# The opening of a hybrid decoder block laid in another order: where the first loads, transposes and small tables stand

## The chip, the cores and the metric

One core of a Trainium2 chip runs the whole kernel. The metric is the device time of one execution in microseconds (us). Three runs of the kernel before took 2296.9, 2298.59 and 2299.16 us; the median is 2298.59. A core has five engines that run their own instruction streams in the order laid down at build time: TensorE (PE; its weight loads are shown apart as PEld), VectorE (DVE), ScalarE (ACT), GpSimd (POOL) and SyncE (SP, which here only asks for transfers). Transfers (DMA) are asked for by SyncE or GpSimd and run beside the engines.

## The reference

One decoder layer over x of 512 tokens by 2048 channels, all float32. Cut to what matters here:

```python
mod = silu(c) @ w_ada + b_ada                # 2048 -> 6 x 2048, one row
shift1, scale1, gate1, shift2, scale2, gate2 = split(mod, 6)
h = rms_norm(x, norm1_w) * (1 + scale1) + shift1
proj = h @ w_in                              # 2048 -> 7168 columns
aq, ak, av, gq, gf, gi, gg = split(proj)     # seven blocks of 1024
attn = dilated_attention(rope(rms(aq)), rope(rms(ak)), av)   # 8 heads
ho = hgrn2(gq, gf, gi, lb)                   # 8 heads, lb from softmax(hg_lb_logits)
x = x + gate1 * (concat(norm(attn), gated(ho)) @ w_out)
x = x + gate2 * (relu(h2 @ w_ff1)**2 @ w_ff2)                # h2: x normalised and modulated again
```

Before any product with `w_in`, x must be normalised by the root mean square of each token, turned so that channels lie on the 128 partitions, and scaled by `norm1_w * (1 + scale1)`. `scale1` itself is a product of a vector with 16 MB of `w_ada`.

## The kernel before

**Precision and products.** Each float32 operand of a large product is split into a rounded part `hi` and a rest `lo`; a product is three matmuls (hi·hi, lo·hi, hi·lo). Weights are split on the fly: ScalarE casts `whi` (L39), VectorE subtracts `wlo` (L40). The input chunk k (128 channels of 512 tokens) is split into `hhi[k]`, `hlo[k]`.

**Opening.** `crow` takes c, norm1_w and b_ada; TensorE turns it (L82), and ScalarE and VectorE make `sc` = silu(c) (L88, L89). Rows of other small vectors go by GpSimd's queue into the tile `rows` (L94 to L97), which shares its place with `crow`; between its clearing (L92) and those requests GpSimd's stream holds the clearing of a part of `wcol` (L107), a tile that a transfer has filled before.

**Modulation rows.** `gemv` (L116) forms one block of `mod`: it asks for pieces of `w_ada` of 256 KB (SyncE, L123) and VectorE multiplies and adds them with `sc` as per-partition scalars into two accumulators (L127, L129). `to_cols` then sums over partitions by TensorE transposes (L149) and ScalarE copies that accumulate (L152); VectorE adds the bias (L167) and forms `norm1_w * (1 + scale1)` (L169) in `g1c`. scale1 has eight blocks of 256 columns, each serving two chunks k; shift1 has four blocks of 512.

**x.** Sixteen pieces of x (`xs[ti][q]`, L255) are asked for behind the eight pieces of scale block 0. Squares are summed on ScalarE, two of sixteen on VectorE (L261, L264); `rx`, the reciprocal root, is a power on GpSimd (L212). All of x is scaled by `rx` (L277 ScalarE, two pieces; L279 VectorE, fourteen) and turned by 64 transposes (L283) into `xnT[0..15]` (L285), all written ahead of the first product.

**First two groups.** `first_groups` (L288) multiplies pairs of chunks with 512 columns of `gf` and 256 of `gq`, 16 chunks by 18 matmuls; before each pair, `scale_block` (L303) runs a block of scale1 and `scaled` (L332) makes `hhi`, `hlo` of the pair. The first products are unshifted: what shift1 adds is made apart by `shift_through` (L744), a `gemv` of `w_in` with shift1. During the second group `shift_block` steps through the blocks of shift1 and then `shifted` (L339) adds it to the chunks. From project(5120) on (L833) TensorE's order is the written one; all else is ordered at build time by a planner that takes instructions as they become ready by its own timeline, earlier written ones first. `issue_after(ins)` lays the instructions of a block behind `ins` on that engine's stream. A pool with n buffers makes a load wait until one is free.

**Small tables.** Behind the last `g1c` step stand `posf`, the transposes of `rows` (L768, L769), the softmax for `lb` (one exp), and sine and cosine for the rotation (L766 to L818), then eight products on GpSimd (`rot_w`, L822). ScalarE loads a function table ahead of the exp and of the sine.

Of the kernel before, what the change touches and what calls it, by code (L numbers as in the profile page):

```python
# [15 lines left out]
P = 128  # L16
# [28 lines left out]
def hybrid_block(ctx, tc, x, c, positions, norm1_w, w_ada, b_ada, w_in, q_norm_w, k_norm_w,  # L45
# [29 lines left out]
    pool.memset(mhalf, -0.5)  # L75
# [10 lines left out]
    dve.tensor_copy(bcol, ps_c[:, 2 * NK:P])  # L86
    sc = const.tile([P, NK], F32, name="sc")
# [28 lines left out]
    def gemv(view, vec, col0, n=512, early=False):  # L116
# [3 lines left out]
        for k0 in range(0, NK, nk):  # L120
            raw = spare.pop(0) if early and spare else slot("araw") if early else gv.tile([P, 512], F32, name="araw", bufs=4)
            raw = raw.rearrange("p (k n) -> p k n", n=n)
            nc.sync.dma_start(raw, view[:, k0:k0 + nk, col0:col0 + n])  # L123
            for k in range(k0, k0 + nk):
                acc = accs[k % 2]
                if k < 2:
                    dve.tensor_scalar(acc, raw[:, k - k0], vec[:, k:k + 1], None, op0=ALU.mult)  # L127
                else:
                    dve.scalar_tensor_tensor(acc, raw[:, k - k0], vec[:, k:k + 1], acc, op0=ALU.mult, op1=ALU.add)  # L129
# [8 lines left out]
    def to_cols(accs, dst):  # L138

        nb = accs[0].shape[1] // P  # L140
        parts = 1 if nb == 4 else 2
        if parts == 1:
            dve.tensor_tensor(accs[0], accs[0], accs[1], op=ALU.add)
        yield
        pc = bank("pc")
        for j in range(nb):
            for u in range(parts):
                c = (j * parts + u) * P
                pe.transpose(pc[:, c:c + P], accs[u][:, j * P:(j + 1) * P], ident)  # L149
        for j in range(nb):  # L150
            c = pc[:, j * parts * P:(j + 1) * parts * P]
            act.activation(c, c, AF.Copy, accum_out=dst[:, j:j + 1])  # L152
# [7 lines left out]
    def mod_cols(kind, b, dst, nw, n=512, early=False):  # L160

        for _ in gemv(ada_v, sc, kind * D + b * n, n, early):
            yield
        nb = n // P
# [3 lines left out]
        if nw is not None:  # L168
            mod_cols.last = dve.scalar_tensor_tensor(d, d, 1.0, nw[:, b * nb:(b + 1) * nb], op0=ALU.add, op1=ALU.mult)  # L169
# [16 lines left out]
    def load_w(view, k0, c0, n=512, eng=None, ahead=True, raws=None):  # L186
        with tc.high_priority() if ahead else ExitStack():
            raw = wr.tile([P, 2, n], F32, name="wraw", tag="raw", bufs=4)
            nc.sync.dma_start(raw, view[:, k0:k0 + 2, c0:c0 + n])
# [20 lines left out]
    def rstd_of(dst, ss, n, inv_n):  # L210
        dve.tensor_scalar(dst, ss, inv_n, EPS, op0=ALU.mult, op1=ALU.add)
        pool.tensor_tensor(dst, dst, mhalf[:, 0:n], op=ALU.pow)  # L212
# [34 lines left out]
    first_scale = mod_cols(1, 0, g1c, n1c, 256, True)  # L247
    for _ in range(8):
# [7 lines left out]
    for q in range(4):  # L256
        for ti in range(NT):
            jk = work("jk")
            with tc.issue_after(sc_ready.ins), tc.issue_after(sig_ready.ins):
                if q == 3 and ti % 2:  # L260
                    dve.tensor_tensor_reduce(jk, xs[ti][q], xs[ti][q], op0=ALU.mult, op1=ALU.add, scale=1.0, scalar=0.0,  # L261
                                             accum_out=ssx[:, ti, q:q + 1])
                else:
                    act.activation(jk, xs[ti][q], AF.Square, accum_out=ssx[:, ti, q:q + 1])  # L264
    dve.tensor_reduce(rx, ssx, axis=AX.X, op=ALU.add)
    rstd_of(rx, rx, NT, 1.0 / D)
    run_all(first_scale)
    second_scale = mod_cols(1, 1, g1c, n1c, 256, True)
# [4 lines left out]
    xnT = []  # L273
    for q in range(4):
        for ti in range(NT):
            if q == 0 and ti % 2 == 0:
                act.activation(xs[ti][q], xs[ti][q], AF.Copy, scale=rx[:, ti:ti + 1])  # L277
            else:
                dve.tensor_scalar(xs[ti][q], xs[ti][q], rx[:, ti:ti + 1], None, op0=ALU.mult)  # L279
        for j in range(4):  # L280
            pt = bank("ptx")
            for ti in range(NT):
                pe.transpose(pt[:, ti * P:(ti + 1) * P], xs[ti][q][:, j * P:(j + 1) * P], ident)  # L283
            t = slot("xnT")
            act.copy(t, pt)  # L285
            xnT.append(t)

    def first_groups(c_f, c_q, before, after):  # L288
# [1131 lines left out]
```

## Time and profile before

The span is the time from the first to the last instruction of one profiled execution; the execution's own time is a little longer.

| what | value |
|---|---|
| median of three runs | 2298.59 us |
| profiled execution, its own time | 2297.95 us |
| its span | 2296.2 us |
| TensorE busy | 2224.9 us (97%) |
| VectorE busy | 1809.9 us (79%) |
| ScalarE busy | 1098.2 us (48%) |
| GpSimd busy | 447.3 us (19%) |
| DMA moved | 598.31 MB, mean 261 GB/s |
| share of the ending chain | PE 60%, DVE 17%, DMA 14%, issue 6% |

A row of the timeline gives start, duration, engine, line, operation, tile written and tiles read, count, and in brackets the idle time ahead of it with what ended it. A group's row gives busy time and the mean of one in ns, then idle time ahead. Busy time of TensorE is that of overlapping matmuls, so one matmul's duration is longer than the distance between two starts.

### The profile page before, as it was taken

The page shows a single profiled execution, that of the slowest core. Times are in us where ns is not written, and L with a number is a line of the kernel's source. Part 1 is how long each engine was busy: PE and PEld are TensorE (multiplying, and loading weights), DVE is VectorE, ACT ScalarE, POOL GpSimd, SP SyncE. Part 2 cuts the span into 40 slices and gives each one's busy share as a digit, 9 for nine tenths or more (in the row PEclk, how much of TensorE's full clock was granted, in tenths as well). Part 3 has the DMA queues.
Part 4 walks back from the last instruction along what each step waited for, and adds up shares of the span by engine and source line. Part 5 has one row for each costly group of instructions (what it writes and reads, how often), then busy time and mean ns, then how long its engine had stood idle before and what let it go on. Part 6 is the DMA issues. An engine that isn't in the chain of part 4 may idle for free.

```text
span 2296.2 us, 33105 instructions
## 1 busy us (share of the span) xinstructions
PE 2224.9 (97%) x11769; PEld 1824.4 (79%) x11769; DVE 1809.9 (79%) x2765; ACT 1098.2 (48%) x1950; POOL 447.3 (19%) x664
## 2 busy tenths in 40 slices
PE   4899999999999999999999999999999999999999
PEld 3787877888778888778887888888888888888887
DVE  6999777677876565668648988988897679967878
ACT  5555434433344454447544556555564333343332
POOL 1000022000230000002232323323332222222221
PEclk9999999999999999999999999999999999999999
DMA  9798455556545256746969799889889987998784
GB/s 327 254 335 315 124 177 156 177 160 207 187 151 184 68 173 225 247 152 217 367 231 383 251 344 347 298 306 386 298 328 390 339 293 260 385 344 291 278 301 164
DMA packets 262582, 598.31 MB, mean 261 GB/s; under 512 B 23220, under 2 KB 43968, under 8 KB 262416
## 3 DMA queue, kind: packets, MB, share of 16 engines
q1 hardware_dynamic: 186800, 332.54, 43.1%
q0 software_dynamic: 70720, 254.21, 30.0%
q10 hardware_dynamic: 4896, 9.44, 1.2%
q8 instruction: 93, 1.52, 0.3%
q14 instruction: 73, 0.60, 0.1%
HBM read 518.49 MB, written 77.61 MB: 260 GB/s over the span
## 4 chain that ended last, share of the span: by engine, by line
PE 60%; DVE 17%; DMA 14%; issue 6%; ACT 2%; POOL 1%; SPq 0%; DVEq 0%; ACTq 0%; POOLq 0%
PE f L1177 9%; PE f L1178 9%; PE f L1176 9%; DMA araw<-in_w_ada_dram 6%; PE prj L198 5%; PE prj L199 5%; PE prj L200 5%; DVE vlo L1161 3%; DVE acc L129 3%; DVE raw L1144 2%; PE f L208 2%; PE f L206 2%; PE f L207 2%; DMA Fl<-f_lod 2%; DVE wlo L40 2%
## 5 line engine op out<-in xcount | busy, mean ns | idle before, releaser
L1160 ACT CAST vhi<-raw 128x1024 fp32r<-128x1024 f32 x392 | 413.4, 1055 | 534.5 <-PE f L1178 416.3
L1161 DVE TENSOR_TENSOR vlo<-raw,vhi 128x1024 fp32r<-128x1024 f32 x392 | 475.5, 1219 | 153.5 <-ACT vhi L1160 152.7
L1177 PE MATMUL f<-vlo,Fh 128*128 128x512 f32 x1376 | 537.1, 390 | 3.9 <-DVE vlo L1161 3.8
L1178 PE MATMUL f<-vhi,Fl 128*128 128x512 f32 x1376 | 535.8, 389 | 0.8 <-DMA Fl<-f_lod 0.8
L1176 PE MATMUL f<-vhi,Fh 128*128 128x512 f32 x1376 | 536.1, 390 | 0.0
L39 ACT CAST whi<-wraw 128x512 fp32r<-128x512 f32 (+1 forms) x368 | 219.8, 601 | 453.2 <-PE prj L200 313.3
L198 PE MATMUL prj<-whi,hi 128*128 128x512 f32 x896 | 364.9, 407 | 1.3 <-ACT gg L701 1.3
L200 PE MATMUL prj<-whi,lo 128*128 128x512 f32 x896 | 351.4, 392 | 0.0
L199 PE MATMUL prj<-wlo,hi 128*128 128x512 f32 x896 | 351.0, 392 | 0.0
L40 DVE TENSOR_TENSOR wlo<-wraw,whi 128x512 fp32r<-128x512 f32 (+1 forms) x368 | 243.2, 665 | 120.9 <-ACT whi L39 118.3
L129 DVE SCALAR_TENSOR_TENSOR acc<-araw,sc,acc 128x512 f32<-128x512 f32 (+1 forms) x392 | 252.7, 672 | 100.5 <-DMA araw<-in_w_ada_dram 99.2
L1177 PEld LDWEIGHTS f<-vlo,Fh 128*128 128x128 f32 x1376 | 258.3, 188 | 63.3 <-DVE vlo L1161 10.0
L1178 PEld LDWEIGHTS f<-vhi,Fl 128*128 128x128 f32 x1376 | 258.3, 188 | 54.8 <-DMA Fl<-f_lod 1.6
L1176 PEld LDWEIGHTS f<-vhi,Fh 128*128 128x128 f32 x1376 | 258.3, 188 | 53.5
L1144 DVE TENSOR_TENSOR raw<-raw,raw 128x1024 f32<-128x1024 f32 x224 | 267.7, 1216 | 4.1 <-DMA raw<-in_w_ff_dram 3.9
L198 PEld LDWEIGHTS prj<-whi,hi 128*128 128x128 f32 x896 | 169.3, 189 | 36.5 <-ACT gg L701 1.6
L200 PEld LDWEIGHTS prj<-whi,lo 128*128 128x128 f32 x896 | 168.9, 188 | 36.7
L199 PEld LDWEIGHTS prj<-wlo,hi 128*128 128x128 f32 x896 | 169.5, 189 | 33.0 <-DVE wlo L40 1.0
L1122 POOL DMA_DIRECT2D Fh<-f_hid x112 | 79.0, 705 | 425.9 <-PE f L1178 410.8
L208 PE MATMUL f<-hi,wlo 128*128 128x512 f32 x256 | 99.8, 390 | 1.3 <-DVE wlo L40 1.3
L206 PE MATMUL f<-hi,whi 128*128 128x512 f32 x256 | 100.2, 391 | 0.0
L207 PE MATMUL f<-lo,whi 128*128 128x512 f32 x256 | 99.6, 389 | 0.0
(311 smaller groups left out, 2917.0 us busy)
## 6 DMA issues: line engine op xcount, KB each, us to landing
raw<-in_w_ff_dram SPq DMA_DIRECT2D x224, 512.0 KB, 9.7
araw<-in_w_ada_dram SPq DMA_DIRECT2D x384, 256.0 KB, 4.3
Fh<-f_hid POOLq DMA_DIRECT2D x112, 512.0 KB, 6.5
Fl<-f_lod POOLq DMA_DIRECT2D x112, 512.0 KB, 7.7
wraw<-in_w_in_dram SPq DMA_DIRECT2D x104, 512.0 KB, 4.1
Fh<-h_hid POOLq DMA_DIRECT2D x60, 512.0 KB, 6.6
Fl<-h_lod POOLq DMA_DIRECT2D x60, 512.0 KB, 7.5
f_hid<-part POOLq DMA_DIRECT2D x48, 512.0 KB, 7.9
```

Source lines behind the costliest of these rows:

```text
L39: nc.scalar.copy(hi, src)
L40: (eng or nc.vector).tensor_tensor(lo, src, hi.bitcast(F32), op=ALU.subtract)
L129: dve.scalar_tensor_tensor(acc, raw[:, k - k0], vec[:, k:k + 1], acc, op0=ALU.mult, op1=ALU.add)
L198: pe.matmul(banks[ti], lhsT=hi[:, ts], rhs=whi, start=first, stop=False)
L199: pe.matmul(banks[ti], lhsT=hi[:, ts], rhs=wlo, start=False, stop=False)
L200: pe.matmul(banks[ti], lhsT=lo[:, ts], rhs=whi, start=False, stop=last)
L1144: dve.tensor_tensor(dst, a, b, op=ALU.subtract)
L1160: act.copy(hi, src)
L1161: split_done.append(dve.tensor_tensor(lo, src, hi.bitcast(F32), op=ALU.subtract))
L1176: pe.matmul(banks[t], lhsT=fh[u][a][:, ts], rhs=whi[:, a], start=first, stop=False)
L1177: pe.matmul(banks[t], lhsT=fh[u][a][:, ts], rhs=wlo[:, a], start=False, stop=False)
L1178: pe.matmul(banks[t], lhsT=fl[u][a][:, ts], rhs=whi[:, a], start=False, stop=end)
```

## The change

Only the opening is touched.

- `xs`, `w_in`: the first pair of weights (`first_weights`) is asked for right behind x on SyncE, its splits laid behind the first scalings of x.
- Modulation rows: scale blocks 1 to 7 and the shift1 blocks are asked for by GpSimd (`eng=pool`). Block 0 stays with SyncE. The requests of block 1 stand behind the power that makes `rx`, those of each later block behind the block before.
- `scale_cols` takes the place of `mod_cols` for scale1: instead of transposes with accumulating copies, TensorE multiplies the accumulators with a column of ones (taken from the widened `mhalf`), and ScalarE forms `g1c` in one step with `n1c` as scale and `b1c` = (b + 1) * norm1_w as bias.
- x is turned two chunks at a time (`x_turned`), two ahead of the first product and two more behind each `scaled` pair; of the sixteen scalings by `rx`, two stay on VectorE and fourteen are ScalarE's.
- Of the sixteen squares, eight are VectorE's.
- The small tables stand behind the third of eight steps of scale block 0, ahead of x in writing order.
- shift1's first steps are laid behind the last multiply-add of scale1, and the loads of `shift_through(4608)` behind the last weights of the second group.
- `scaled` makes `hhi` straight from the unscaled chunk, ahead of the scaled chunk.

```diff
-    pool.memset(mhalf, -0.5)
+    pool.memset(mhalf[:, 0:16], -0.5)
+    pool.memset(mhalf[:, 16:32], 1.0)
+    ones = mhalf[:, 16:17]
...
+    b1c = bcol[:, NK:2 * NK]
+    dve.scalar_tensor_tensor(b1c, b1c, 1.0, n1c, op0=ALU.add, op1=ALU.mult)
...
-    def gemv(view, vec, col0, n=512, early=False):
+    def gemv(view, vec, col0, n=512, early=False, eng=None):
...
-            nc.sync.dma_start(raw, view[:, k0:k0 + nk, col0:col0 + n])
+            gemv.load = (eng or nc.sync).dma_start(raw, view[:, k0:k0 + nk, col0:col0 + n])
...
+    def scale_cols(b):
+        steps = gemv(ada_v, sc, D + b * 256, 256, True, pool if b else None)
+        for _ in range(NK // 2):
+            with ExitStack() as order:
+                for ins in scale_cols.behind:
+                    order.enter_context(tc.issue_after(ins))
+                next(steps)
+            yield
+        next(steps, None)
+        scale_cols.behind = [gemv.last.ins, gemv.load.ins]
+        accs = gemv.acc
+        scale_cols.last_dve = gemv.last
+        pc = bank("pc")
+        for j in range(2):
+            for u in range(2):
+                pe.matmul(pc[:, j:j + 1], lhsT=accs[u][:, j * P:(j + 1) * P], rhs=ones, start=u == 0, stop=u == 1)
+        for j in range(2):
+            ks = slice(2 * b + j, 2 * b + j + 1)
+            scale_cols.last = act.activation(g1c[:, ks], pc[:, j:j + 1], AF.Identity, scale=n1c[:, ks],
+                                             bias=b1c[:, ks])
+        yield
+    def mod_cols(kind, b, dst, nw, early=False):
+        for _ in gemv(ada_v, sc, kind * D + b * 512, 512, early, pool if early else None):
+            yield
...
-    first_scale = mod_cols(1, 0, g1c, n1c, 256, True)
-    for _ in range(8):
+    first_scale = scale_cols(0)
+    scale_cols.behind = []
+    for _ in range(3):
+        next(first_scale)
+    posf = ca.tile([NT, P], F32, name="posf")
...
+            pool.tensor_tensor(rot_w[:, i, j], tab, w, op=ALU.mult)
+
+    for _ in range(5):
         next(first_scale)
...
-                if q == 3 and ti % 2:
+                if ti % 2:
                     dve.tensor_tensor_reduce(jk, xs[ti][q], xs[ti][q], op0=ALU.mult, op1=ALU.add, scale=1.0, scalar=0.0,
...
+    def x_turned(k, anchor):
+        q, j = k // 4, k % 4
+        if j == 0:
+            for ti in range(NT):
+                if q == 0 and ti % 2:
+                    x_turned.dve = dve.tensor_scalar(xs[ti][q], xs[ti][q], rx[:, ti:ti + 1], None, op0=ALU.mult)
+                else:
+                    with tc.issue_after(anchor.ins):
+                        x_turned.act = act.activation(xs[ti][q], xs[ti][q], AF.Copy, scale=rx[:, ti:ti + 1])
+        pt = bank("ptx")
+        for ti in range(NT):
+            pe.transpose(pt[:, ti * P:(ti + 1) * P], xs[ti][q][:, j * P:(j + 1) * P], ident)
+        t = slot("xnT")
+        act.copy(t, pt)
+        xnT.append(t)
+    for k in range(2):
+        x_turned(k, last_square)
...
+    with tc.issue_after(x_turned.act.ins), tc.issue_after(x_turned.dve.ins):
+        first_weights = [pair_of_weights(0, 4096, 3072)]
+    second_scale = scale_cols(1)
...
+    scale_cols.behind += [rx_ready.ins, x_turned.dve.ins]
...
-            wt = load_w(win_v, k0, c_f, ahead=False)
-            wc = load_w(win_v, k0, c_q, 256, None, ahead=False)
+            wt, wc = first_weights.pop() if first_weights else pair_of_weights(k0, c_f, c_q)
...
-            run_all(mod_cols(1, k0 // 2 + 1, g1c, n1c, 256, True))
+            run_all(scale_cols(k0 // 2 + 1))
         for k in (k0, k0 + 1):
             scaled(k)
+        for k in range(k0 + 2, min(k0 + 4, NK)):
+            x_turned(k, scaled.last)
     def shift_start(k0):
         if k0 == 14:
-            for _ in range(12):
-                bg_step()
+            with tc.issue_after(scale_cols.last_dve.ins):
+                for _ in range(12):
+                    bg_step()
...
+        scaled.last = act.activation(hhi[k], xnT[k], AF.Copy, scale=g1c[:, k:k + 1])
         act.activation(xnT[k], xnT[k], AF.Copy, scale=g1c[:, k:k + 1])
-        act.copy(hhi[k], xnT[k])
...
-    with tc.issue_after(mod_cols.last.ins):
-        posf = ca.tile([NT, P], F32, name="posf")
...
-    later.insert(0, shift_through(4096 + 512))
+    later.insert(0, behind(shift_through(4096 + 512), load_w.last.ins))
```

More of the change, by code (lines that the diff above doesn't have):

```diff
@@ L244, in hybrid_block @@
     hhi, hlo, spare = [], [], []
-    first_scale = mod_cols(1, 0, g1c, n1c, 256, True)
-    for _ in range(8):
+    first_scale = scale_cols(0)
[3 more added lines that the diff above has]
+    posf = ca.tile([NT, P], F32, name="posf")
+    dve.tensor_copy(posf, posi)
+    ps_v = bank("ps_v")
+    pe.transpose(ps_v[:, 0:P], rows, ident)
+    pe.transpose(ps_v[:, P:P + NT], posf, ident[0:NT, 0:NT])
+    dve.tensor_copy(cols[:, 0:41], ps_v[:, 0:41])
+    dve.tensor_copy(posc, ps_v[:, P:P + NT])
@@ new lines, in hybrid_block @@
+    dve.reciprocal(lbm, lbm)
+    dve.tensor_tensor(lb, lbe[:, 0:8], lbm, op=ALU.mult)
+    dve.tensor_scalar(omlb, lb, -1.0, 1.0, op0=ALU.mult, op1=ALU.add)
+    rot_w = ca.tile([P, 2, 4, NT, 16], F32, name="rot_w")
+    cosT, sinT = (work(n)[:, 0:NT * 16].rearrange("p (t f) -> p t f", f=16) for n in ("cosT", "sinT"))
+    rp = work("rp")
+    ang, rem, half, co = (rp[:, i * 64:(i + 1) * 64] for i in range(4))
+    for ti in range(NT):
+        dve.tensor_scalar(ang[:, ti * 16:(ti + 1) * 16], ifq, posc[:, ti:ti + 1], None, op0=ALU.mult)
```

166 lines of the change are left out of this document (71 added, 95 removed).

## The prediction

> **What bounds the kernel now.** The page's first line, then a table of busy time by windows in five stretches cut where the work changes: x coming in, the first product group (L761), the second (L824), the start of project(5120), the rest.
>
> ```profile
> span 2296.2 us, 33105 instructions
> ```
>
> ```profile
> core 0: us, PE busy (x) PEld busy (x) DVE busy (x) ACT busy (x) POOL busy (x), PEclk, DMA share, GB/s
> 0.00:29.49 29.49, 1.74 (x5) 0.86 (x5) 11.77 (x35) 12.05 (x36) 9.64 (x24) 1.00 0.90 296
> 29.49:121.60 92.11, 82.75 (x380) 66.98 (x381) 85.39 (x228) 54.22 (x118) 0.00 (x0) 0.96 0.83 271
> 121.60:187.20 65.60, 65.60 (x296) 53.98 (x294) 63.32 (x116) 37.30 (x86) 4.75 (x8) 1.00 1.02 367
> 187.20:220.00 32.80, 27.93 (x116) 22.30 (x116) 31.77 (x54) 18.86 (x44) 0.53 (x1) 0.90 0.99 356
> 220.00:2296.20 2076.20, 2046.90 (x10977) 1680.30 (x10975) 1617.64 (x2336) 975.73 (x1670) 432.40 (x631) 1.00 0.73 255
> ```
>
> TensorE is the bound from 220 on and in the second group, which is full. All that the beginning can return lies before 220: 27.8 us idle while x comes in, a first group that takes 92.1 us where the second, with as many products, takes 65.6, and 4.9 idle before 220. TensorE's waits up to 300 us name the places (total, times, longest):
>
> ```profile
> PE ptx L283 <- ACT xs L277: 12.8, 1, 12.8
> PE pc L149 <- DVE acc L129: 12.4, 3, 11.4
> PE prj L206 <- ACT hi L336: 6.9, 3, 4.1
> PE pc L149 <- DVE acc L143: 4.9, 1, 4.9
> ```
>
> In order of time:
>
> ```profile
> 25.89 0.69 DVE L261 CUSTOM_DVE_ANT_0 jk<-xs 128x512 f32<-128x512 f32 x1 [0.69 <-ACT jk L264]
> 26.50 0.08 DVE L261 DVE_READ_ACCUMULATOR2_ANT ssx<- 128x1 f32 x1
> 27.48 1.21 POOL L212 TENSOR_TENSOR rx<-rx,mhalf 128x4 f32<-128x4 f32 x1 [14.29 <-DVE rx L211]
> 29.49 5.59 PE L283 MATMUL ptx<-ident,xs 128*128 128x128 f32 x28 [12.77 <-ACT xs L277]
> 36.80 1.21 PE L206 MATMUL prj<-hi,whi 128*128 128x512 f32 x4 [0.90 <-ACT hi L336]
> 43.13 1.91 PE L283 MATMUL ptx<-ident,xs 128*128 128x128 f32 x16
> 94.20 2.08 PE L206 MATMUL prj<-hi,whi 128*128 128x512 f32 x4 [4.06 <-ACT hi L336]
> ```
>
> ```profile
> 208.93 0.39 PE L200 MATMUL prj<-whi,lo 128*128 128x512 f32 x1
> 214.17 1.11 PE L149 MATMUL pc<-ident,acc 128*128 128x128 f32 x4 [4.86 <-DVE acc L143]
> ...
> 216.36 0.63 PE L198 MATMUL prj<-whi,hi 128*128 128x512 f32 x1
> 216.79 0.63 PE L199 MATMUL prj<-wlo,hi 128*128 128x512 f32 x1
> ```
>
> The rows' scale rx is ready at 28.7; the first product starts 8.1 us later, behind 28 transposes; at 94 and 214 TensorE waits 4.1 and 4.9 us for work of VectorE, and restarts slowly (starts 0.43 apart at 216). The 214 wait is VectorE's backlog: from 28.72 to 214.1 it is busy 175.7 of 185.4 us, and the gap lies after 107, when the queue of SyncE stands with weight loads that wait for buffers and the modulation rows behind them:
>
> ```profile
> 28.72:214.10 185.38, 170.46 (x770) 138.46 (x770) 175.74 (x389) 106.53 (x234) 5.29 (x9) 0.98 0.92 317
> 107.20:125.60 18.40, 18.40 (x82) 15.03 (x81) 11.47 (x50) 12.61 (x23) 0.41 (x2) 1.00 0.48 153
> ```
>
> ```profile
> 90.20 29.70 SPq L189 DMA_DIRECT2D wraw<-in_w_in_dram  x7
> 119.96 9.72 SPq L123 DMA_DIRECT2D araw<-in_w_ada_dram  x13
> ```
>
> So two clocks must both improve: TensorE's own work from rx on, and VectorE's from rx to 214.
>
> **1. When rx is ready.** The small tables move ahead of x's squares, and six more squares move from ScalarE to VectorE. The tables need the tile rows:
>
> ```profile
> 10.62 0.09 POOL L107 MEMSET wcol<- 32x2 f32 x1 [3.34 <-DMA wcol<-in_k_norm_w_dram]
> ...
> 12.70 0.48 POOL L97 DMA_DIRECT2D rows<-in_hg_norm_w_dram  x1
> ```
>
> ```profile
> rows<-in_hg_norm_w_dram POOLq DMA_DIRECT2D x1, 0.5 KB, 4.8
> ```
>
> Nothing in the diff asks for rows sooner, so its last part lands at 12.7 + 4.8 = 17.5; with transpose and copy (some 0.7, estimated from the 0.39 of a product and the copy's 0.2 below) VectorE can begin at 18.2. The tables' 38 VectorE instructions run from L766 to L818:
>
> ```profile
> 107.30 0.21 DVE L766 CAST posf<-posi 4x128 f32<-4x128 int32 x1
> ...
> 114.04 0.20 DVE L770 COPY cols<-ps_v 128x41 f32<-128x41 f32 x1 [0.99 <-PE ps_v L769]
> ...
> 125.41 0.20 DVE L818 TENSOR_SCALAR cosT<-rp 128x64 f32<-128x64 f32 x1
> ```
>
> ```profile
> L40 DVE TENSOR_TENSOR wlo<-wraw,whi 128x512 fp32r<-128x512 f32 x28 | 19.2, 686 | 2.4 <-ACT whi L39 2.1 <-PE pc L149 0.3
> L40 DVE TENSOR_TENSOR wlo<-wraw,whi 128x256 fp32r<-128x256 f32 x27 | 11.1, 415 | 2.0 <-ACT whi L39 2.0
> L337 DVE TENSOR_TENSOR lo<-xnT,hi 128x512 fp32r<-128x512 f32 x16 | 10.7, 682 | 0.0
> ```
>
> Their cost: 11.47 us busy in that stretch less four large and four small weight splits and two lo (4 x 0.69 + 4 x 0.42 + 2 x 0.68 = 5.8) leaves 5.7 (38 x 0.2 = 7.6 at most). Eight squares cost 8 x (0.69 + 0.08) = 6.2, sum and scale 0.3, the power 1.2. Block 0's sixteen multiply-adds cost 0.4 each, by this row:
>
> ```profile
> 55.90 3.24 DVE L129 SCALAR_TENSOR_TENSOR acc<-araw,sc,acc 128x256 f32<-128x256 f32 x8
> ```
>
> An engine runs its instructions in the order laid down. If only the six written ahead of the tables go before the copy at 18.2, rx comes at 18.2 + 5.7 + 10 x 0.4 + 6.2 + 0.3 + 1.2 = 35.6. If all sixteen and two squares go ahead: 18.2 + 5.7 + 4.6 + 0.3 + 1.2 = 30.0. If the tables fit into gaps, 28.2 (x's last piece on VectorE at 25.9 at the latest, and no wait for ScalarE's scratch). I take **33.5**, nearer the first: the tables are written before block 0's last ten steps and all squares, and rows is late. Behind the waiting copy stand those steps and squares; for the squares everything waits. rot_w on GpSimd (eight products, the 4.75 us of the second group's row) can stand ahead of the power as well; as the squares end after the tables, I count nothing for it.
>
> **2. TensorE from rx to the end of group one.** The floor is the second group's 65.6, 64 transposes at 1.91 / 16 = 0.12 = 7.6, and the column sums. Those now are matmuls with one moving column, 32 for scale; no row shows one. Between nothing and a transpose (3.8 in all) I take 2. Together 75.2; before spent 92.1, so 16.9 us over its floor. What remains: 3 from the first transpose to a steady stream (eight transposes instead of 28, ScalarE's copies and casts ahead of the first hi), and 3 for waits pair by pair, since VectorE's load per pair is close to TensorE's: 16 x 0.4 + 2 x 0.69 + 2 x 0.42 + 2 x 0.68 = 10.0 (less where they overlap) against 75.2 / 8 = 9.4. So 6 over, bounds 3 and 12. No shift step stands between scale steps any more (all are laid behind the last scale step), which removes the cause that I read into the wait at 94. Group one then ends at 33.5 + 0.8 + 75.2 + 6 = 115.5 instead of 121.6. ScalarE gains 12 scalings of x and loses accumulating copies; with 54 of 92 us busy it has room. The first weights behind x cost and gain nothing of their own: the wait at 36.8 names hi, not weights.
>
> **3. VectorE from rx to the wait at 214.** 175.7, less 12 scalings of x and the g1c steps, less tables, plus six steps of block 1 that before did ahead of 28.72:
>
> ```profile
> 32.84 2.46 DVE L279 TENSOR_SCALAR xs<-xs,rx 128x512 f32<-128x512 f32 x6
> ...
> 48.73 0.15 DVE L167 TENSOR_TENSOR g1c<-g1c,bcol 128x2 f32<-128x2 f32 x1
> 48.80 0.61 DVE L127 TENSOR_SCALAR acc<-araw,sc 128x256 f32<-128x256 f32 x2
> ```
>
> 175.7 - 12 x 0.41 - 16 x 0.1 - 5.7 + 6 x 0.4 = 165.9. Idle time: 3 at the start (GpSimd's first request goes out after the power, so block 1 lands later than now) and 3 after; bounds 3 and 16. The modulation rows no longer queue behind SyncE's weights, so the idle stretch after 107 should go. VectorE is through at 33.5 + 165.9 + 6 = 205.4. TensorE arrives 87.7 after group one (209.3 - 121.6), at 203.2, waits 2.2 and goes on at 205.4 instead of 214.2: 8.8 gained.
>
> **The clock.** After 4.06 and 4.86 us idle, products start 0.43 apart (216.36 to 216.79) where the second group needs 65.6 / 296 = 0.22 for one; I estimate nine such gaps after 214, the first 4 us of it, 1.8 us in all. The wait of 2.2 I count without that, so 1.8 more. [...]
>
> **Sum.** 8.8 + 1.8 = 10.6. The profiled execution took 2297.95 (span 2296.2); 2297.95 - 10.6 = **2287.4**, called 2287. The median of the runs, 2298.6, stands 0.6 above the profiled one; I add nothing for that.
>
> **Rivals.** *Tables hide*: rx at 28.2. Group one ends at 110.2, TensorE arrives at 197.9, VectorE at 200.1; gain 14.1 + 1.8 = 15.9, 2282. For it: VectorE is idle 17.7 of the first 29.5 us. Against: rows at 17.5.
>
> *Backlog stays*: group one is quicker, but VectorE idles 16 us instead of 6, because GpSimd's in-order requests wait for buffers, as SyncE's did; it is through at 215.4, TensorE waits 12, and the gain is given back: 2299. For it: in the second group VectorE is busy 63.3 of 65.6 with DMA at 367 GB/s, so little can be caught up. Against: rows have their own queue.
>
> *GpSimd asks too slowly* (the other side): eight requests a block must fit into 9.4 us, so it decides from 1.17 us a request. SyncE spaced 13 in 9.72 = 0.75 apart (the row at 119.96); GpSimd's requests late in this kernel take
>
> ```profile
> L1122 POOL DMA_DIRECT2D Fh<-f_hid x112 | 79.0, 705 | 425.9 <-PE f L1178 410.8
> ```
>
> for 512 KB, beside a busy VectorE. At 1.5 (twice SyncE's) a block takes 12: seven blocks lose 7 x 2.6 = 18, group one ends at 133.5, TensorE arrives at 221.2, the four shift blocks' 64 requests (96 us) end about then, and it goes on 7 to 15 us later than at 214.2: 2309. [...]
>
> *It does not do what it says*: if the order laid down puts rx later than 39.6, group one ends no earlier than now (39.6 + 0.8 + 81.2 = 121.6); this I count with the backlog case.
>
> **How the numbers follow.** Main case 0.42 (own range 2281 to 2294: rx 30 to 35.6, VectorE idle 3 to 8), tables hide 0.26, backlog 0.19, slow requests 0.13. A measurement can tell about 0.2%, 4.6 us: faster is below 2294, slower above 2303.2. Faster: 0.42 + 0.26, same 0.19, slower 0.13. The range runs from 2276 (the second case with no excess, 6 us less) to 2302 (the backlog case and 3).
>
> **What would show it.** The copy of cols on VectorE at about 18 with squares after it, and the power's end at 30 to 36: part 1. First product 4 to 5 us after that; group one's banks read at 113 to 118; no 4 us wait in it: part 2. [...] GpSimd's requests above 1.17 us, or VectorE waiting for araw longer than 3 us at a time, would make me wrong, as would new waits of TensorE after 220, which I take to be unchanged.

## The result, and the profile after

The kernel after the change takes 2324.52 us (median of four runs, 2323.21 to 2330.62) against 2298.88 us of the kernel before (2296.9 to 2300.74): a ratio of 1.0117, 95% interval 1.0097 to 1.0137. It is slower by 1.2%, and lies outside the predicted range of 2276 to 2302. The profiled execution is the longest of the four: 2330.62 us, of which the span is

```profile
span 2328.9 us, 33185 instructions
```

Busy time by windows of the kernel after, cut at the same events as the table of before (first turns of x, end of group one, end of group two, the restart in project(5120)):

```profile
core 0: us, PE busy (x) PEld busy (x) DVE busy (x) ACT busy (x) POOL busy (x), PEclk, DMA share, GB/s
0.00:34.35 34.35, 2.88 (x11) 2.32 (x11) 20.93 (x78) 11.12 (x27) 15.74 (x34) 1.00 0.73 244
34.35:141.30 106.95, 95.31 (x409) 74.85 (x409) 76.06 (x171) 59.64 (x115) 47.50 (x71) 0.92 0.71 229
141.30:208.65 67.35, 67.20 (x301) 54.97 (x299) 57.81 (x104) 33.48 (x79) 27.00 (x50) 1.00 0.96 341
208.65:246.00 37.35, 27.27 (x104) 22.05 (x105) 35.69 (x59) 21.21 (x48) 0.53 (x1) 0.82 0.97 349
```

The opening is 4.9 us longer than before (34.35 against 29.49), as the early tables were expected to make it. Group one is 14.8 us longer (106.95 against 92.11), and that was not expected. Group two is full as before. Behind it TensorE idles 10 us of 37. Up to their last cuts (246.00, and 220.00 before) the two profiled executions are 26.0 us apart, at their ends 32.7; the 6.7 us between are not explained here, and the medians differ by 25.6. In group one VectorE, which the prediction took to be the tight engine, is busy 76 of 107 us; before it was 85 of 92, some 10 of them tables and scalings of x that the change moves away. TensorE's longest waits from the first turns up to 300 us (total, times, longest):

```profile
PE pc L151 <- DVE acc L145: 7.0, 1, 7.0
PE pc L188 <- DVE acc L133: 5.4, 7, 1.6
PE prj L241 <- ACT hi L449: 4.5, 6, 1.9
PE prj L233 <- ACT f L854: 3.1, 1, 3.1
```

No wait of 4 us stands in group one any more; thirteen short ones for column sums and hi stand there, one or two for each pair of chunks, and four for lo (1.4 us in all). The events that the prediction named, from the timeline:

```profile
18.70 0.20 DVE L292 COPY cols<-ps_v 128x41 f32<-128x41 f32 x1 [2.56 <-PE ps_v L291]
25.53 0.68 DVE L359 CUSTOM_DVE_ANT_0 jk<-xs 128x512 f32<-128x512 f32 x1
32.59 1.04 POOL L247 TENSOR_TENSOR rx<-rx,mhalf 128x4 f32<-128x4 f32 x1 [1.85 <-DVE rx L246]
34.45 1.97 PE L380 MATMUL ptx<-ident,xs 128*128 128x128 f32 x8 [13.98 <-ACT xs L377]
38.28 2.07 PE L241 MATMUL prj<-hi,whi 128*128 128x512 f32 x4 [1.86 <-ACT hi L449]
139.23 1.58 ACT L854 ACTIVATE f<-prj 128x512 f32<-128x512 f32 x3 [1.42 <-PE prj L243]
211.70 0.50 PE L233 MATMUL prj<-whi,hi 128*128 128x512 f32 x1 [3.05 <-ACT f L854]
240.15 1.11 PE L151 MATMUL pc<-ident,acc 128*128 128x128 f32 x4 [7.04 <-DVE acc L145]
```

rx is ready at 33.6 and the first product starts at 38.3, both as forecast. Group one's banks are read from 139.2 (forecast: 113 to 118). The wait for VectorE that stood at 214 now stands at 240 and is longer.

One passage from pair to pair in group one of the kernel after shows where the time is. TensorE:

```profile
88.23 0.39 PE L243 MATMUL prc<-hi,wlo 128*128 128x512 f32 x1
89.23 0.38 PE L188 MATMUL pc<-mhalf,acc 128*128 128x1 f32 x2 [0.61 <-DVE acc L133]
89.48 0.63 PE L380 MATMUL ptx<-ident,xs 128*128 128x128 f32 x4
89.96 0.83 PE L188 MATMUL pc<-mhalf,acc 128*128 128x1 f32 x6
90.79 0.66 PE L380 MATMUL ptx<-ident,xs 128*128 128x128 f32 x4
92.09 1.63 PE L241 MATMUL prj<-hi,whi 128*128 128x512 f32 x4 [0.65 <-ACT hi L449]
```

ScalarE and VectorE in the same passage:

```profile
90.15 0.59 ACT L382 COPY xnT<-ptx 128x512 f32<-128x512 f32 x1 [1.31 <-PE ptx L380]
90.83 0.59 ACT L191 ACTIVATE g1c<-pc,bcol,n1c 128x1 f32<-128x1 f32 x2
91.32 0.72 ACT L449 ACTIVATE hi<-xnT,g1c 128x512 fp32r<-128x512 f32 x1
93.16 0.69 DVE L451 TENSOR_TENSOR lo<-xnT,hi 128x512 fp32r<-128x512 f32 x1 [3.25 <-ACT xnT L450]
```

After the last product of a pair (88.23) come, one behind the other: the end of the next scale block on VectorE, its column sums, the two turns of x for this very pair, ScalarE's copy, its scale, its hi, and only then the next product. That is 3.5 us (88.6 to 92.1). VectorE stands in front of lo for 3.25 us (89.91 to 93.16), and the multiply-adds of the block after next are behind lo in its list. So the blocks cannot run ahead, and from 75 us on the passage comes again for each pair, five times: first lo of the pairs at 66.25, 79.62, 93.16, 106.19, 120.22 and 133.62, some 13.5 us apart where the forecast had 9.4 for TensorE. VectorE's group of lo in the kernel after, and the windows from 34 to 140 us, after and then before:

```profile
L451 DVE TENSOR_TENSOR lo<-xnT,hi 128x512 fp32r<-128x512 f32 x16 | 10.9, 691 | 23.5 <-ACT xnT L450 23.2
34.00:140.00 106.00, 94.02 (x403) 73.78 (x404) 75.36 (x170) 58.69 (x112) 46.79 (x69) 0.92 0.71 228
```

```profile
34.00:140.00 106.00, 96.65 (x444) 77.69 (x443) 97.00 (x249) 61.87 (x139) 4.75 (x8) 0.97 0.85 282
```

Before, the same group's idle time was 0.0, and VectorE was busy 97 of these 106 us.

### The profile page after: what moved, and what is told of

It reads as the page before. It is cut to its first block, busy times and chain, and to the rows that moved or that the text cites. A ratio compares the mean times of both kernels' runs of the same rounds, so it can differ in the third digit from the quotient of the medians.

```text
span 2328.9 us, 33185 instructions
## 1 busy us (share of the span) xinstructions
PE 2246.4 (96%) x11801; PEld 1839.6 (79%) x11801; DVE 1812.3 (78%) x2750; ACT 1101.1 (47%) x1934; POOL 523.1 (22%) x785
## 3 DMA queue, kind: packets, MB, share of 16 engines
q0 software_dynamic: 80320, 285.68, 33.6%
## 4 chain that ended last, share of the span: by engine, by line
PE 62%; DVE 14%; DMA 12%; issue 8%; POOL 2%; ACT 2%; SPq 0%; DVEq 0%; ACTq 0%; POOLq 0%
PE f L1231 9%; PE f L1232 9%; PE f L1230 9%; PE prj L233 6%; PE prj L235 6%; PE prj L234 6%; DMA araw<-in_w_ada_dram 6%; DVE vlo L1215 3%; DVE acc L133 2%; PE f L243 2%; PE f L241 2%; PE f L242 2%; DMA f_lod<-fs 2%; DVE raw L1198 2%; PE prj L242 1%
```

## The experiments

All ratios are to the kernel before, run on the same chip in the same series; the medians of before were 2294.6 to 2300.6 us in these series. In the diffs a minus line is the kernel after, unless said otherwise. The theories at the start were: the order on VectorE (lo ahead of the next block), GpSimd's requests, the early tables, and the turning of x pair by pair.

**sp_rows.** The rows are asked for by SyncE again.

```diff
-        steps = gemv(ada_v, sc, D + b * 256, 256, True, pool if b else None)
+        steps = gemv(ada_v, sc, D + b * 256, 256, True, None)
...
-        for _ in gemv(ada_v, sc, kind * D + b * 512, 512, early, pool if early else None):
+        for _ in gemv(ada_v, sc, kind * D + b * 512, 512, early, None):
```

> Only the requests of the modulation rows go back from GpSimd to SyncE. Three theories of the 25 us. (1) The loop: in group one VectorE's list has lo (line 451) of a pair ahead of the multiply-adds of the next scale block, lo waits for ScalarE's xnT (line 450), xnT waits for the scale made of the block before, and so the blocks can't run ahead; 13.4 us a pair against the 9.4 of TensorE. This edit leaves lo where it is in the list, so the loop theory expects the banks of group one read within 3 us of 139.2 and 2318 to 2330 us. (2) GpSimd's requests come too late, because its list waits for free buffers: then the next block's rows are there sooner, the pairs come at some 10 us, the banks are read from 120 or so and the time is 2298 to 2308. (3) the tables or the turning of x: no change, as (1).

Measured: 2315.67 us, 1.0080 (1.0061 to 1.0099); banks read from 136.1. A part of the loss at most, neither all nor clearly nothing: the interval just touches that of the kernel after (1.0097 to 1.0137).

**lo_behind.** lo laid behind a part of the next block's steps in VectorE's list.

```diff
-        dve.tensor_tensor(hlo[k], xnT[k], hhi[k].bitcast(F32), op=ALU.subtract)
+        with tc.issue_after(scale_cols.mid.ins) if k < 14 else ExitStack():
+            dve.tensor_tensor(hlo[k], xnT[k], hhi[k].bitcast(F32), op=ALU.subtract)
```

Here `scale_cols.mid` is the last multiply-add of the block's fourth step.

> The kernel after the change, except that lo of each pair but the last is laid behind the fourth of eight steps of the next scale block in VectorE's list. Requests, tables and the turning of x pair by pair stay. Loop theory: the wait of lo for xnT (38 us in the window 33 to 145) mostly goes, the pairs come at 9.5 to 11 us, the banks are read from 116 to 125, and the time falls by 12 to 22 us, to 2302 to 2312. If the requests of GpSimd or the turning of x in the loop of TensorE and ScalarE set the pace, VectorE only waits at another line: banks within 4 us of 139.2, time 2316 to 2330.

Measured: 2335.34 us, 1.0161 (1.0142 to 1.0179); banks read from 143.5. The wait for xnT did go (from 23.2 us, not the 38 of the expectation, to 2.2), and the time went the other way. VectorE's waits from 33 to 145 us in this kernel:

```profile
DVE wlo L40 <- ACT whi L39: 30.1, 17, 2.9
DVE lo L454 <- ACT xnT L452: 2.2, 4, 0.7
```

It now waits for the casts of the weights, which wait for TensorE (41.7 us of ScalarE's waits), and TensorE waits 15.8 us for lo instead of 1.4. The edit makes lo late for its own pair, so by itself it does not settle my first theory. Two runs below do: pc_one leaves lo's place as it is, and its wait for xnT is down to 4.0 us; before_pairs has the loss without any such wait.

**x_at_once.** All of x scaled and turned ahead, as in the kernel before.

```diff
-                if q == 0 and ti % 2:
+                if q or ti % 2:
                     x_turned.dve = dve.tensor_scalar(xs[ti][q], xs[ti][q], rx[:, ti:ti + 1], None, op0=ALU.mult)
...
-    for k in range(2):
+    for k in range(NK):
         x_turned(k, last_square)
...
-        for k in range(k0 + 2, min(k0 + 4, NK)):
-            x_turned(k, scaled.last)
```

> All of x is scaled and turned ahead of the first product, 14 of the 16 later scalings on VectorE, as before the change; the requests by GpSimd and the early tables stay. In VectorE's list lo of pair 0 comes two steps into the next block and lo of the following pairs a block or more later, so the loop is open. Loop theory and the theory that the turning in the loop costs the time expect the same here: first product later by 8 to 12 us than 38.3, pairs at 9.4 to 10.5, banks read from 118 to 128, time 2300 to 2312. GpSimd's requests as the cause: banks still after 133, time over 2315.

Measured: 2297.07 us, 0.9995 (0.9984 to 1.0006). The whole loss is gone with this one part undone. Its timeline, and its window from 34 to 140:

```profile
34.21 4.59 PE L380 MATMUL ptx<-ident,xs 128*128 128x128 f32 x24 [13.99 <-ACT xs L377]
38.56 1.18 PE L241 MATMUL prj<-hi,whi 128*128 128x512 f32 x4
114.93 0.60 ACT L852 ACTIVATE f<-prj 128x512 f32<-128x512 f32 x1 [0.28 <-PE prj L243]
118.44 0.60 ACT L852 ACTIVATE f<-prj 128x512 f32<-128x512 f32 x1
208.88 0.66 PE L151 MATMUL pc<-ident,acc 128*128 128x128 f32 x4 [1.74 <-DVE acc L145]
```

```profile
34.00:140.00 106.00, 102.90 (x501) 85.80 (x502) 97.38 (x216) 61.68 (x129) 59.01 (x91) 1.00 0.89 300
```

I had expected the first product 8 to 12 us later; it came at 38.56 instead of 38.28. The planner lays 24 transposes ahead of it, while ScalarE and VectorE make hi, and the rest behind the first products. Turning in pairs bought 0.3 us at the start, and lost them at once: the first four products take 2.07 us in the kernel after and 1.18 here. The `prj` banks are read from 114.9 to 118.4.

**tables_late.** The tables back behind the scale columns: the same lines, moved behind `scale_cols.last_dve` with `issue_after`.

> Only the tables (positions, rotary, layer scales) go back to their place behind the scale columns. rx is ready about 5 us sooner (28 to 30 instead of 33.6). Loop theory: everything up to the end of group one moves by these 5 us at most, since lo stands ahead of the next block as before: banks read from 133 to 138; the tables' 7 us then lie behind group one on VectorE, so the time is 2318 to 2330. If the tables were the cause: 2300 to 2310.

Measured: 2327.37 us, 1.0127 (1.011 to 1.0144), not to be told from the kernel after. The first product came 4 us sooner (34.27) and the banks were read from 134.1, so the opening's 5 us came back and were lost behind group two, where TensorE then waited 12.7 us for VectorE. The tables are not the cause.

**pc_one.** The column sums of all blocks share one bank. In group one the four `prj` banks and the two `prc` banks stay taken, so two of the pool's banks are left for `pc` and the `ptx` of a pair.

```diff
-        pc = bank("pc")
+        if b == 0:
+            scale_cols.pc = bank("pc")
+        pc = scale_cols.pc[:, 2 * b:2 * b + 2]
```

> The kernel after the change, except that the sums of the scale columns (pc, line 188) of all eight blocks share one PSUM bank of their own instead of taking a bank each time. New theory, the banks: in group one the four prj banks and the two prc banks are held throughout, so that two of eight banks are left, which pc and the two ptx of a pair take in turn; the second ptx of a pair needs the bank of that block's pc, so it stands behind the end of the block (89.23 pc, 89.48 ptx, 89.96 pc, 90.79 ptx), and column, turn and pair go in lock step at 13.4 us. With a bank for pc alone the scale blocks can run ahead: banks of group one read from 116 to 126 instead of 139.2, time 2298 to 2311. If the turning itself (its place right ahead of its own pair, its copies and scalings on ScalarE) costs the time: read after 134, time 2316 to 2330.

Measured: 2306.81 us, 1.0027 (1.0013 to 1.0041); banks read from 129.4. Three quarters of the loss are gone, with x still turned in pairs; group one is still slower than with x at once.

```profile
34.00:140.00 106.00, 97.08 (x446) 78.16 (x447) 84.29 (x186) 62.51 (x122) 53.03 (x80) 0.97 0.79 263
```

**lead_two.** Each turn two pairs ahead of its use: `range(4)` ahead of the first product, `range(k0 + 4, min(k0 + 6, NK))` in the loop.

> The kernel after the change, except that x is turned two pairs ahead of its use instead of one (four columns of x ahead of the first product). Theory that the turn comes too late for its pair: hi no longer waits for it, the gap between two pairs shrinks from 3.5 to under 2 us, banks read from 118 to 127, time 2298 to 2311. Theory of the banks: pc and ptx still share two banks, the block still ends right ahead of its pair, banks read after 131 and 2314 to 2330.

Measured: 2318.23 us, 1.0086 (1.0063 to 1.0109); banks read from 141.1. Not to be told from the kernel after, or little better: that the turn comes late for its pair is not the cause, or little of it.

**scaled_ahead.** All scalings of x ahead, 14 of 16 on VectorE, turns in pairs.

```diff
+    for q in range(4):
+        for ti in range(NT):
+            if q or ti % 2:
+                x_turned_dve = dve.tensor_scalar(xs[ti][q], xs[ti][q], rx[:, ti:ti + 1], None, op0=ALU.mult)
...
```

> The kernel after the change, except that all of x is scaled at once, 14 of 16 pieces on VectorE, ahead of the first product; the turning stays pair by pair. If the scalings on ScalarE (2.5 us a quarter of x, three times in group one) cost the time: banks read from 120 to 130, time 2300 to 2314. Theory of the banks: still in lock step, later by the 6 us of the scalings on VectorE or less: banks read from 136 to 145, time 2318 to 2334.

Measured: 2333.25 us, 1.0150 (1.0135 to 1.0165); banks read from 138.1. The scalings on ScalarE were not the cause.

**x_at_once_sp.** x_at_once and sp_rows together.

> x turned all at once and the requests of the modulation rows by SyncE: of the change the early tables, the new column sums and the order of weights and shift steps are left. If GpSimd's requests cost by themselves what they cost in the kernel after the change (2324.5 with, 2315.7 without): 2286 to 2292, faster than both kernels. If they cost only where the pairs go in lock step: within 3 us of 2297.

Measured: 2296.79 us, 0.9989 (0.9978 to 1.0). The same as x_at_once (0.9995): with x turned at once GpSimd's requests cost nothing that can be told, where with the pairs in step sp_rows stood at 1.0080 against 1.0117.

**before_pairs.** The kernel before with one part of the change (a minus line is the kernel before here).

```diff
-        for j in range(4):
-            pt = bank("ptx")
+    def x_turned(k):
+        q, j = k // 4, k % 4
+        pt = bank("ptx")
...
+    for k in range(2):
+        x_turned(k)
...
         for k in (k0, k0 + 1):
             scaled(k)
+        for k in range(k0 + 2, min(k0 + 4, NK)):
+            x_turned(k)
```

> The kernel before, with the turning of x alone put pair by pair as the change has it (all scalings stay ahead, requests by SyncE, tables late, old column transposes). Theory of the banks: here too two of eight banks are left to the columns' pc and the ptx, the scale blocks fall in step with the pairs, and the kernel becomes slower by 12 to 30 us: 2311 to 2330, banks of group one read after 130 instead of 119. If the loss needs the other parts (GpSimd's requests, early tables, new columns): 2296 to 2305.

Measured: 2322.99 us, 1.0109 (1.0092 to 1.0126); banks read from 138.9. The one part alone brings the loss, in a kernel that has nothing else of the change. Its window, its waits for hi up to 300 us, and what VectorE waits for most from 34 to 140 us:

```profile
34.00:140.00 106.00, 89.50 (x370) 70.21 (x371) 77.05 (x197) 49.61 (x110) 0.00 (x0) 0.90 0.68 218
```

```profile
PE prj L206 <- ACT hi L343: 10.5, 5, 2.5
DVE acc L127 <- DMA araw<-in_w_ada_dram: 9.0, 6, 3.1
```

VectorE's 97 us of work in this window have become 77, close to the 75 of the kernel after. Here the rows, which SyncE asks for, come late; in the kernel before VectorE had no wait for them in this window.

**pc_one_sp.** pc_one and sp_rows together.

> The kernel after the change with the one pc bank and the rows asked for by SyncE; x stays pair by pair. The bank alone gave 2306.8. If the rest of it is GpSimd's requests: 2296 to 2300. If the rest is the turning in the loop (one bank for all turns, their copies in ScalarE's list): 2303 to 2309.

Measured: 2316.07 us, 1.0082 (1.0066 to 1.0097): no better than sp_rows without the bank, and worse than pc_one with GpSimd. Both expectations missed. VectorE's wait from 34 to 140 us that pc_one hardly had (1.9 us there):

```profile
DVE acc L131 <- DMA araw<-in_w_ada_dram: 8.2, 3, 4.8
```

Once the bank is out of the way, SyncE's rows are late. I read this as one link of the loop opened and the next one holding.

**once_sp_early.** x_at_once_sp with `if k0 == 12` for `if k0 == 14` in `shift_start`.

> x turned at once, rows by SyncE, and the first twelve steps of the shift columns written one pair sooner (behind pair 12 instead of pair 14). In the run without this VectorE sat idle 6.6 us between 118 and 126 for rows and for weights, and TensorE waited 3.9 us at 210 for VectorE. If the idle time comes from the late writing of these steps: the wait at 210 goes, 2288 to 2294. If the steps only take the place of the scale blocks' work: 2294 to 2300.

Measured: 2296.87 us, 0.9995 (0.9985 to 1.0005), no difference.

**once_sp_pc, and again as once_sp_pc_b.** x_at_once, sp_rows and pc_one together.

> x turned at once, rows by SyncE, and one bank for all scale columns. With x turned ahead pc has two banks to itself for most of group one, so the theory of the banks expects nothing from it: within 3 us of 2296.8. If the one bank helps by something else than the lock step (as by column reads that wait): under 2293.

> The kernel with x at once, rows by SyncE and one pc bank again, in more rounds: 2294.9 the first time. It should stand at 2292 to 2297, under the kernel before by 2 to 5 us.

Measured: 2294.93 us, 0.9984 (0.9973 to 0.9996), and in a second series 2289.76 us, 0.9982 (0.9969 to 0.9995). It beats both kernels, the kernel before by 0.2%, at the edge of what can be told; both intervals lie under 1. Against x_at_once_sp (0.9989) the bank alone makes no difference that can be told, as expected.

**slots_held.** x_at_once, but a quarter of x keeps its buffers up to the pair at which the change would free them.

```diff
+        if k0 % 4 == 0:
+            with tc.issue_after(scaled.last.ins):
+                for ti in range(NT):
+                    act.copy(held[:, k0 // 4, ti:ti + 1], xs[ti][k0 // 4][:, 0:1])
```

> x turned all at once, rows by GpSimd, but each quarter of x keeps its four buffers until the pair at which the change would give them up: a one-column read of each piece on ScalarE is written there (16 reads more, nothing else). This has the change's hold on the row buffers without its turning inside the loop and without pc and ptx meeting in the two banks. If the buffers held by x are the cause of the 25 us or of much of it: banks of group one read after 128, 2308 to 2325. If the banks and the turning in the loop are: 2296 to 2304.

`held` is a small tile that nothing reads. Measured: 2294.38 us, 0.9997 (0.9987 to 1.0007).

**slots_held_sp.** The same with SyncE's requests.

> The same with the rows asked for by SyncE, whose list also holds the weights' loads. With turning pair by pair and SyncE, a bank for pc gave nothing (2315.7 without, 2316.1 with), while VectorE waited 8 us for rows. If x's held buffers keep SyncE's list waiting there: this one is slow too, 2306 to 2318, with waits of VectorE for rows of 5 us and more. If not: 2294 to 2301.

Measured: 2291.83 us, 0.9984 (0.9973 to 0.9996). Buffers held that long by themselves cost nothing.

**lead_two_pc.** lead_two and pc_one together.

> The kernel after the change with one bank for pc and x turned two pairs ahead. One bank for pc left 2306.8, with one other bank for all turns; there hi and lo still waited 3 us and the turns 3 us for each other. If what is left is that a turn comes too late for its pair: 2296 to 2303. If it is the work of the turns in the loop and x's held buffers: 2303 to 2312.

Measured: 2310.22 us, 1.0068 (1.0055 to 1.0081): slower than pc_one alone (1.0027). Turning earlier does not add to the bank; it takes from it.

**turns_twice.** x_at_once, and 14 turns done again in the loop, into a bank that ScalarE reads over; their results are not used.

```diff
+    def turned_again(k):
+        pt = bank("ptx")
+        for ti in range(NT):
+            pe.transpose(pt[:, ti * P:(ti + 1) * P], xs[ti][k // 4][:, k % 4 * P:(k % 4 + 1) * P], ident)
+        act.activation(pt, pt, AF.Copy, accum_out=held[:, k:k + 1])
```

> x turned all at once ahead (2297.1 as it was), and in group one 14 of the 16 turns done a second time, pair by pair where the change has them, into a bank that ScalarE reads over and nobody uses (56 transposes and 14 reads more; no product waits for them). TensorE's extra work is 14 times some 0.63 us, 9 us. If the column sums and the turns hold each other up in the two banks, whoever needs the turned x: the scale blocks fall in step, 2310 to 2326. If the loss is that hi waits for a turn that comes late: only the extra work shows, at most 2306.

Measured: 2317.12 us, 1.0073 (1.0058 to 1.0088).

**turns_twice_pc.** The same with one bank for the sums.

> The same with one bank for all column sums, so that sums and turns no longer share. Theory of the banks: 7 to 18 us under the one without, 2297 to 2308. If the turns' own work and their reads in the loop cost the time: the same as without within 4 us.

Measured: 2315.58 us, 1.0064 (1.0047 to 1.008). Against x_at_once (0.9995) the second turns cost 0.8%, 18 us, of which their own work on TensorE is at most 9 (14 x 0.63), with 14 reads on ScalarE beside it; no product waits for them. A bank for the sums changes nothing here, against the theory of the banks and as the other expectation had it. What VectorE waits for in turns_twice, from 34 to 145 us:

```profile
DVE wlo L40 <- ACT whi L39: 9.9, 9, 2.6
DVE acc L133 <- DMA araw<-in_w_ada_dram: 9.4, 7, 2.7
DVE acc L131 <- DMA araw<-in_w_ada_dram: 2.6, 2, 2.3
```

The rows are late by 12 us in sum, which slots_held had at 4.2 and x_at_once not at all. The rows use the buffers that x gives up; in slots_held ScalarE's read gives them up beside hi of the pair, here a transpose does, and TensorE's list may have it behind a pair's 36 products. GpSimd's requests do wait 6.7 us for the second turns in turns_twice, where in x_at_once they wait 0.9 for the turns; but in turns_twice_pc it is 2.7 us, with about the same loss. So this is one way at most, read from the waits; no run took it alone.

What is shown: the turning of x inside group one, pair by pair, is the cause of the loss, in the kernel after (taken out: 0.9995) and in the kernel before (put in: 1.0109). That a turn in the loop costs time although no product needs it is shown by turns_twice. How it costs it is read from lists and waits: sums, turns and products of one pair come behind each other in TensorE's list, and VectorE gets 20 us less done from 34 to 140 (before_pairs against the kernel before). What holds the pairs seems to depend on the rest: the shared banks with GpSimd's requests (18 us back), late rows with SyncE's (nothing back). Moving lo, the scalings, or the turn one by one gave nothing or little. What makes up the 6 to 8 us that pc_one still loses stays open.

## Why the prediction was wrong, point by point

**rx at 33.5: right**, 33.63 measured. The parts differ: block 0's sixteen steps all went ahead of the copy at 18.7, not six, and no square did. For that order the prediction's own terms give 18.2 + 5.7 + 6.2 + 0.3 + 1.2 = 31.6. A copy 0.5 later, tables of 6.8 us (18.70 to 25.53) for 5.7 and a wait of 0.85 for ScalarE's last square, less squares 0.73 apart for 0.77, make up the other 2. The value between the two cases was hit by luck.

**First product 4 to 5 us behind rx: right**, 4.7. But the reason was not the eight transposes in place of 28: with x at once it starts at 38.56.

**Group one, 6 us over its floor of 75.2: this step failed.** By the same sum, with the first product of group two at 141.30 (141.30 - 33.63 - 0.8 - 75.2), the excess is 31.7. Of its two terms, "3 from the first transpose to a steady stream" came out up to the first product (3.83 less the eight transposes, 0.96); "3 for waits pair by pair" is the one that failed. From 34.35 to 141.30 TensorE idles 11.6 us, and is busy 95.3 instead of 75.2: 8.5 instead of 2 are the column sums, and some 9 the lower clock, an estimate from the 0.92 of that window (0.08 x 107). The few us left I cannot sort. I priced the pairs by VectorE's load against TensorE's, 10.0 to 9.4, as if the two could overlap freely, and counted the 64 transposes as 7.6 us of work that could stand anywhere. I did not follow what a turn inside the loop waits for and who waits for it, though the change moves it between the column sums and hi of its own pair. My rival for waits of that kind named the requests alone. The column sums were a term of the floor sized wrong: 2 us in all. Their group in the kernel after, from 34 to 140 us:

```profile
L188 PE MATMUL pc<-mhalf,acc 128*128 128x1 f32 x56 | 8.5, 256 | 5.4 <-DVE acc L133 5.4
```

A block's four matmuls stand as eight records, 56 in seven blocks, busy for 8.5 us; where all eight stand together, as in pc_one, they take 0.95 us. Even 7 x 0.95 = 6.7 is more than the 28 transposes that they replace, which were busy for 5.1 us in group one of the kernel before. With the turning undone the step holds, within its bounds of 3 and 12: in x_at_once rx is ready at 33.40 and group two's first product starts at 119.49, 10.1 over the floor that I had set.

**VectorE through at 205.4 with a wait of 2.2: wrong through the same step**, 240.15 and 7.04. Its work was forecast rightly, 165.9 us (164.6 measured from 33.63 to 240.15); its assumed idle time of 6 us became some 40 (133.9 busy of the 174.3 us from 34.35 to 208.65 already). With the turning undone it is 208.88 and 1.74. The sum's 1.8 us for the clock take it that no slow products follow a wait of 2.2 us; no run shows that term. In its place the runs showed: behind 1.74 us in x_at_once products 0.23 apart from 209.60 on, at a clock of 1.00 (200 to 220); in the kernel after 0.43 apart behind 3.05 us (212.39 to 215.38) and behind 7.04 us (241.48 to 246.18, at a clock of 0.50 from 240 to 246).

**Nothing new behind 220: wrong too.** Even x_at_once, whose first 209 us go nearly as forecast (restart at 208.88, 5.3 us ahead of the kernel before), takes 2297.07 against 2298.26 in its series, only 1.2 less. ScalarE begins a stretch of `gq<-f` (L798; L686 in the kernel before) at 313.31 against 319.89, 6.6 us ahead, and a later one at 608.35 against 609.90, 1.5 ahead. TensorE's waits from 215 to 620 us, in x_at_once and then in the kernel before:

```profile
PE pC L760 <- DVE z L713: 3.8, 3, 2.0
PE ptq L566 <- ACT p_sb L604: 2.7, 1, 2.7
PE pB L686 <- DVE z L713: 2.5, 3, 1.5
```

```profile
PE pC L648 <- DVE z L601: 3.0, 2, 2.8
PE ptq L454 <- ACT p_sb L492: 2.0, 1, 2.0
PE pB L574 <- DVE z L601: 1.0, 1, 1.0
```

Over the whole lists the waits come to 10.6 us against 6.4, 4.2 more, 2.8 of them where the steps of the recurrence (`hgrn2`) on VectorE, tile z, hold TensorE; the lead shrinks by 5.1 between those two stretches. Why those steps hold TensorE longer is not shown.

**The rivals.** GpSimd asking too slowly has the right sign and a time (2309) nearer than my forecast, but not its mechanism: requests took 0.54 to 0.81 us, under the 1.17 from which it decides, and sp_rows gives back about a third of the loss, at the edge of what can be told, x_at_once_sp nothing. The backlog rival was right in that VectorE idles, wrong in what for. That the tables hide was excluded by the copy at 18.7.

## What to carry to other kernels

Before moving work from ahead of a loop into it, write down one turn of that loop as a chain over the engines' lists (here VectorE stood 3.25 us in front of lo, with the multiply-adds of a later block behind it), with what each moved instruction waits for, whose buffer or bank it needs, and what stands behind it; loads that balance say nothing while the chain is closed (10.0 to 9.4 us a pair here, with the pairs 13.5 apart). Work that is laid out ahead may cost nothing at the start, if the planner can put it beside the first products (first product at 38.56 with it, 38.28 without). When one link of such a chain is opened and the time stays, look for the next link in the waits, and undo the move as a whole to know what it costs.

## What the runs showed of the hardware

In one passage of the kernel after TensorE's granted clock fell to 0.57 with no wait over 0.65 us in the 3.5 us ahead of it. Windows of the kernel after around the passage shown above and around the next one:

```profile
88.62:92.09 3.47, 2.21 (x17) 1.81 (x17) 1.29 (x4) 2.06 (x6) 1.45 (x2) 1.00 0.55 178
92.09:96.07 3.98, 3.98 (x10) 3.15 (x11) 2.76 (x7) 2.38 (x4) 0.72 (x1) 0.57 0.27 97
96.07:101.90 5.83, 5.83 (x27) 4.70 (x25) 5.59 (x14) 1.65 (x3) 3.62 (x5) 1.00 0.75 200
101.90:105.11 3.21, 2.36 (x18) 1.77 (x16) 1.16 (x4) 2.22 (x6) 0.55 (x1) 1.00 0.94 332
105.11:107.00 1.89, 1.72 (x7) 1.11 (x7) 0.81 (x2) 1.89 (x4) 1.89 (x4) 1.00 0.68 191
```

In 3.47 us TensorE was busy for 2.21, with sixteen small matmuls, and its longest wait was 0.65; the next 4 us ran at 0.57 of the clock, products 0.43 apart, and then at 1.00 again, 0.23 apart. That passage so costs about 1.7 us more (0.43 x 3.98), an estimate. The next one, of 3.21 us with TensorE busy for 2.36 and a longest wait of 0.52, was followed by products at 1.00 of the clock: not every passage has this price. From 34 to 140 us the clock was 0.92, where x_at_once had 1.00. The prediction had read slow products only behind single waits, of 4.06 and 4.86 us; here they came behind several short ones. What lowers the clock behind one passage and not behind the next is not shown.

GpSimd's requests for the rows took 0.54 to 0.81 us each in the kernel after (120 requests, VectorE busy 76 of 107 us in group one), never more, and cost nothing that could be told when x was turned at once (0.9995 with them, 0.9989 without).
